# Two DMAs at the seam between attention and the za product: the last attention store on SyncE's queue, and the first gate loads ahead of two bulk loads

## The chip, the cores and the metric

The kernel runs on one core of a Trainium2 chip. The core has TensorE (PE, matrix products), VectorE (DVE, elementwise work), ScalarE (ACT, activations and copies), GpSimd (POOL) and SyncE (SP), each with its own in-order stream of instructions, and 16 DMA engines that all of them feed. DMAs are issued here by SyncE and by POOL, for the most part. The metric is the time of one execution on the device, in microseconds (us), as the median of several runs.

## The reference, cut to what matters

One layer of a hybrid encoder, 1024 tokens by 1024 channels, all in float32:

```python
h = rmsnorm(x, norm_g)
q, k, v, za, u, vs, zs, gm = split(h @ w_in)
a = window_sink_attention(rope(q), rope(k), v, sinks)      # 16 heads, 2 key heads, 128-frame window
a = (a * silu(za)) @ w_att_out
s = chunked_spatial_gating(gelu(u), gelu(vs), ...)
s = (s * silu(zs)) @ w_sg_out
ga, gs = split(sigmoid(gm + b_merge))
out = rmsnorm(x + (ga * a + gs * s) @ w_o, final_g)
```

The change touches the place where the attention result `a` is handed to `a * silu(za)`.

## The kernel before, in words

**Products.** Every large product is computed with feature rows on the 128 partitions and 1024 tokens in two halves of 512. It uses Strassen's scheme on 2 by 2 blocks: seven block products for a pair of 128-row output tiles instead of eight. A value is split into a high and a low part (`wh`, `wl` for weights, `T_...h`, `T_...l` for the other operand), and each block product is 12 matmuls of 128x128 by 128x512 (`product`, L362). One call of `gemm_pair` (L371) makes one pair of output tiles: the seven products stand in the order b11, t1, t2, b21, t3, b22, t4, and behind each one a `hook()` is called, so a pair has hooks 1 to 7. Between the products ACT copies partial results out of PSUM into tiles named `x` (L380, L384, L387), DVE adds the next partial results to them (L392, L397, L401), and `split_next` splits the next weights: high part on ACT (L176), low part on DVE (L177). There are five `x` tiles in rotation, and a pair uses four.

**Stages around the change.** The products for z (the SiLU path of the gating branch), gs and ga are made first, and the attention, cut into small steps, runs from their hooks. Each of the 16 attention tiles is (g, t): half the heads g by a block of 128 tokens t. `value_stage` (L1535) ends a tile: ACT and DVE bring it into `aT` (L1559, L1560), and POOL issues its store into the DRAM scratch `at_dr` (L1562). After the last of them the memory of the attention's tiles is given back, and a new pool, `later`, is laid over it. It holds four bulk tiles `bq` of 128 x 2048 values and the gate tiles `g0`, `g1`, later also `g2`, `g3`.

Then come four pairs for za (m = 0, 2, 4, 6; two by `gemm_pair`, two by a variant that keeps partial sums in PSUM). Each of their hooks calls `part_of_s`, which does two jobs side by side:

- It makes the operand of the following product, silu(z) times the spatial gating result. `parts_of_s` (L1767) returns a schedule written out by hand: a dictionary from (m, hook) to the steps to be issued there. `load` brings a quarter of z into a bulk tile (1024 KB, `bq<-z_dr`), `load_factors` a quarter of the gating result (1024 KB, `bq<-s_dr` in the traces), `load_row` one 128-row piece of it, `silu` works on ACT (L1787), `multiply` on DVE (L1791).
- It makes the za operand. When a quarter-tile of za is complete, ACT applies SiLU (L1857). `finish_silu` (L1837) multiplies it on DVE by the matching tile of the attention result (L1744), has POOL store it to the DRAM scratch `a_dr` (L520), and asks for the next gate. A **gate** here is that tile of the attention result, read back from `at_dr` (256 KB, `g<-at_dr`) by `want_gate` (L1756) into a free gate tile. The first two are asked for by the step `first_gates` (L1803); every later one needs a gate tile that a multiply has released.

`copy_to` (L211) issues on SyncE; all loads of this stage go that way, and the instruction shown for them is L212. SyncE handles its entries in order, so a load that must wait holds up those behind it.

**What sets the order.** The program is recorded as written and then planned: for each engine a fixed order is chosen from the dependences, the order of writing and estimated durations, and semaphores are placed. `after(b, a)` (L99) adds an order by hand; the gate multiplies stand so behind the latest partial sum (`term`), and the SiLU steps behind the latest ACT copy (`pace`).

Of the kernel before, what the change touches and what calls it, by code (L numbers as in the profile page):

```python
# [52 lines left out]
def hybrid_tile(  # L53
# [16 lines left out]
    nc = tc.nc  # L70
# [12 lines left out]
    def bank(tag, dt=F32):  # L83
        return psum.tile([P, 512], dt, name=nm("ps_" + tag), tag="ps_" + tag, bufs=2)
# [14 lines left out]
    def after(second, first):  # L99

        tc.add_manual_dep(
            second.ins,
            first.ins.name,
            mybir.DependencyInfo(mybir.DependencyClass.NoSync, mybir.DependencyReason.DATA),
            reason="order",
        )
# [104 lines left out]
    def copy_to(dst, src):  # L211
        nc.sync.dma_start(dst, src)  # L212
# [39 lines left out]
    def half_of(half):  # L252
        return slice(half * HALF, (half + 1) * HALF)
# [198 lines left out]
    def of_w(i0, i1):  # L452
        return lambda dst, i, j: copy_to(dst, w[(i0, i1)[i]][:, half_of(j)])

    def of_token_w(base, m):


        def load(dst, i, j):
            first, c0 = base + 4 * ((m + i) // 4) + 2 * j, ((m + i) % 4) * P
            d = dst.rearrange("p (c k n) -> p c k n", c=2, k=2)  # L460
            for c in range(2):
                copy_to(d[:, c], w[first + c].rearrange("p (k n) -> p k n", k=2)[:, :, c0 : c0 + P])

        return load
# [8 lines left out]
    for base, step in ((W_U, 1), (W_Q, 0), (W_ZS, 1), (W_SG, 2), (W_ATT, 2)):  # L473
        if base == W_Q:
            jobs.append(pair_job(len(jobs), of_kv))
        for m in range(0, KC, 2):
            load = of_w(base + step * m, base + step * (m + 1)) if step else of_token_w(base, m)
# [44 lines left out]
    def get(src, m, half, bufs, tag="g"):  # L522
        g = mtile([P, HALF], F32, tag, bufs, pool)
        copy_to(g[:], place(src, m, half))
        return g
# [820 lines left out]
    steps = [(g, t, par) for g in range(2) for t in range(NT) for par in range(2)]  # L1346
# [61 lines left out]
    def atile(shape, dt, tag, bufs):  # L1408
        return mtile(shape, dt, tag, bufs, pool)
# [125 lines left out]
    def value_stage(g, t, par, parts):  # L1535


        if par == 0:
            keys[g, t][3] = atile([P, 4, P], F32, "aT", 2)
        _, va, vb, at = keys[g, t]  # L1540
        a, b = parts
        po = bank("o")
        vs = slice(par * HD, par * HD + P)
        first = slice(0 if t else 256, 512)
        for n in range(2):
            nc.tensor.matmul(  # L1546
                po[:, first], va[1][:, vs], a[:, n, first], start=n == 0, stop=n == 1, skip_group_check=True
            )
        for c in range(2 if t else 1):
            cs = slice(256 * c, 256 * c + 256)  # L1550
            nc.tensor.matmul(
                po[:, cs], vb[c][:, vs], b[c][:], start=t == 0, stop=True, skip_group_check=True
            )
        here, there = slice(HD * par, HD * (par + 1)), slice(HD * (1 - par), HD * (2 - par))
        out_of, dst = (
            lambda half: po[half].rearrange("p (c i q) -> p c i q", c=2, i=4),
            at[here].rearrange("p i (c q) -> p c i q", c=2),
        )
        nc.scalar.copy(dst, out_of(there))  # L1559
        nc.vector.tensor_add(dst, dst, out_of(here))  # L1560
        if par == 1:
            nc.gpsimd.dma_start(  # L1562
                at_dr[:].rearrange("(c p) t -> p c t", p=P)[:, 4 * g : 4 * g + 4, t * P : (t + 1) * P], at[:]
            )

# [2 lines left out]
    def attention():  # L1568
# [9 lines left out]
        def value(n):  # L1578
            value_stage(*steps[n], weights.pop(0))
            if n % 2 and n + 3 < len(steps):  # L1580
                value_loads(*tiles[n // 2 + 2])
# [63 lines left out]
    def bq(n=None):  # L1645
        if n is None:
            n_bq[0] += 1
        return mtile([P, 4, HALF], F32, f"bq{(n_bq[0] if n is None else n) % 4}", 1, pool)
# [92 lines left out]
    def times(v, by, minus):  # L1741
        if minus:
            return nc.vector.scalar_tensor_tensor(v, v, -1.0, by, op0=ALU.mult, op1=ALU.mult)
        return nc.vector.tensor_mul(v, v, by)  # L1744
# [11 lines left out]
    def want_gate(src, m, half):  # L1756
        tag = free_tags.pop(0)
        gates.append((tag, get(src, m, half, 1, tag)))
# [8 lines left out]
    def parts_of_s():  # L1767

        factors, of_rows = [], {}

        def rows(src, j, half):
            return src[:].rearrange("(c p) t -> p c t", p=P)[:, 4 * j : 4 * j + 4, half_of(half)]

        def load(j, half):
            s_q[j, half] = q = bq()
            copy_to(q[:], rows(z_dr, j, half))

        def load_factors(j, half):  # L1780
            factors.append(bq(0))
            copy_to(factors[-1][:], rows(s1_dr, j, half))

        def silu(j, half):
            for c in range(0, 4, 2):
                v = s_q[j, half][:, c : c + 2, :]
                after(nc.scalar.activation(v, v, AF.Silu), pace[0])  # L1787

        def multiply(j, half, c):
            v = s_q[j, half][:, c : c + 2, :]  # L1790
            after(nc.vector.tensor_mul(v, v, factors[-1][:, c : c + 2, :]), term[0])  # L1791

        def load_row(c, half):
            of_rows[c, half] = get(s1_dr, 4 + c, half, 1, f"g{2 + c % 2}")

        def multiply_row(c, half):
            v = s_q[1, half][:, c, :]
            move = times(v, of_rows[c, half][:], half == 0)
            after(move, term[0])
            if half == 0 and c > 1:  # L1800
                late_rows.append(move)

        def first_gates():  # L1803
            for _ in range(2):
                want_gate(at_dr, *of_att.pop(0))

        def more_gates():
            free_tags.extend(("g2", "g3"))
            for _ in range(2):
                want_gate(at_dr, *of_att.pop(0))  # L1810

        return {
            (0, 1): [(load, 0, 0), (load_factors, 0, 0)],
            (0, 2): [(load, 1, 1)],
            (0, 3): [(load, 0, 1), (first_gates,)],
            (0, 4): [(load_row, 0, 1), (load_row, 1, 1)],
            (0, 5): [(silu, 0, 0)],
            (0, 6): [(multiply, 0, 0, 0)],
            (0, 7): [(multiply, 0, 0, 2), (load_factors, 0, 1), (silu, 1, 1)],
            (2, 1): [(multiply_row, 0, 1), (multiply_row, 1, 1), (load_row, 2, 1), (load_row, 3, 1)],  # L1820
            (2, 3): [(silu, 0, 1)],
            (2, 6): [(multiply, 0, 1, 0), (multiply_row, 2, 1)],
            (2, 7): [(multiply, 0, 1, 2), (multiply_row, 3, 1), (load, 1, 0), (load_row, 0, 0), (load_row, 1, 0)],
            (4, 6): [(silu, 1, 0)],
            (4, 7): [(multiply_row, 0, 0), (multiply_row, 1, 0), (load_row, 2, 0), (load_row, 3, 0)],
            (6, 2): [(multiply_row, 2, 0), (multiply_row, 3, 0), (more_gates,)],
        }


    of_att = [(m + i, half) for m in range(0, KC, 2) for i, half in ORDER]  # L1830
    s_q = {}
    making_s = parts_of_s()
    of_za = [0]

# [191 lines left out]
    for p in range(4):  # L2026
        n, t, acc, x11 = N_PAIRS + p, T_ORDER[p], accs[p], firsts[p]
# [191 lines left out]
```

## Time and profile before

| | |
|---|---|
| time, median of 3 runs | 897.91 us (896.01 to 897.95) |
| span of the profiled execution | 895.1 us |
| time of the profiled execution itself | not on the page |
| PE, matmuls | 883.5 us busy (99%), 4117 matmuls |
| PE, weight loads | 730.8 us (82%) |
| DVE / ACT / POOL | 685.0 (77%) / 580.7 (65%) / 152.2 us (17%) |
| DMA | 212.40 MB, mean 237 GB/s |

The span runs from the first to the last instruction of one execution, and the time of a run is measured around it, so it is somewhat longer. A busy PE means that matmuls are under way; their ends are modelled. In the views, "a<-b" is output<-input by the names in the program, "x12" a count, and a wait is put down to whatever released it. SPq stands for SyncE's queue of DMA issues: its durations are the issue alone, not the transfer.

### The profile page before, as it was taken

Reading aid. Unit: us, or ns where it says so; the run is one execution under the profiler, and the core shown is the slowest. Engines: PE = TensorE matmul, PEld = TensorE weight load, DVE = VectorE, ACT = ScalarE, POOL = GpSimd, SP = SyncE. Lnnn points to the kernel's source line nnn. Section 1 sums busy time; section 2 is a strip of 40 time slices with the busy share of each in tenths; the row PEclk is TensorE's granted clock in tenths of the full one; section 3 lists DMA queues with packets and bytes.
Section 4 is the critical chain, followed back from the end, with each engine's and each line's share of the span. In section 5 each row is a group of like instructions: output and inputs, shape, how many; then the busy total and the mean of one; then the engine's idle time right before and its main releaser. Section 6 shows DMA issues by size and latency. Waiting matters only on the chain.

```text
span 895.1 us, 13162 instructions
## 1 busy us (share of the span) xinstructions
PE 883.5 (99%) x4117; PEld 730.8 (82%) x4117; DVE 685.0 (77%) x1362; ACT 580.7 (65%) x1189; POOL 152.2 (17%) x218
## 2 busy tenths in 40 slices
PE   9999999999999999999999999999999999999997
PEld 6888888888888888888888888887888888888886
DVE  7879966566686778888878888846796588479886
ACT  6875523334445489999989999964685375467443
POOL 3322222203030011111211011101121121110012
PEclk9999999999999999999999999999999999999999
DMA  9998888858778767887776689989899789998523
GB/s 333 216 280 207 270 202 172 172 159 266 245 247 299 205 186 188 210 196 192 179 234 216 228 225 229 243 297 336 313 286 385 284 227 255 307 294 283 189 105 131
DMA packets 130962, 212.40 MB, mean 237 GB/s; under 512 B 12778, under 2 KB 59370, under 8 KB 130892
## 3 DMA queue, kind: packets, MB, share of 16 engines
q1 hardware_dynamic: 108280, 148.36, 49.9%
q0 software_dynamic: 22464, 62.93, 31.4%
q8 instruction: 33, 0.54, 0.2%
q14 instruction: 37, 0.30, 0.1%
q10 hardware_dynamic: 148, 0.27, 0.1%
HBM read 146.37 MB, written 86.11 MB: 260 GB/s over the span
## 4 chain that ended last, share of the span: by engine, by line
PE 90%; issue 3%; ACT 3%; DMA 2%; DVE 1%; SPq 0%; POOL 0%; ACTq 0%; POOLq 0%
PE ps_mm L362 39%; PE ps_o L362 25%; PE ps_tp L362 6%; PE ps_sc L362 3%; PE ps_o L793 3%; PE ps_tp L793 2%; PE ps_mm L793 2%; PE ps_sc L1438 2%; PE ps_tp L1511 2%; PE ps_tp L1109 2%; PE ps_o L1546 2%; PE ps_sc L793 1%; DMA a_dr<-x 1%; DMA wr<-in_x_dram 1%; PE ps_sc L663 1%
## 5 line engine op out<-in xcount | busy, mean ns | idle before, releaser
L176 ACT CAST wh<-s 128x1024 fp32r<-128x1024 f32 (+1 forms) x79 | 79.4, 1007 | 75.9 <-PE ps_mm L362 27.6
L177 DVE TENSOR_TENSOR wl<-wr,wh 128x512 fp32r<-128x512 f32 (+1 forms) x77 | 72.1, 938 | 60.0 <-ACT wh L176 59.1
L177 DVE TENSOR_TENSOR wl<-s,wh 128x1024 fp32r<-128x1024 f32 (+1 forms) x79 | 92.6, 1173 | 9.7 <-ACT wh L176 9.5
L176 ACT CAST wh<-wr 128x512 fp32r<-128x512 f32 (+1 forms) x77 | 63.0, 819 | 54.6 <-PE ps_mm L362 31.6
L362 PE MATMUL ps_o<-T_t1h,wh 128*128 128x512 f32 x148 | 57.8, 391 | 0.0
L362 PE MATMUL ps_o<-T_t1h,wl 128*128 128x512 f32 x148 | 57.7, 390 | 0.0
L362 PE MATMUL ps_o<-T_t1l,wh 128*128 128x512 f32 x148 | 57.6, 389 | 0.0
L362 PE MATMUL ps_mm<-T_t3h,wh 128*128 128x512 f32 x140 | 55.0, 393 | 2.0 <-ACT x L387 2.0
L1444 ACT COPY sl<-ps_sc 128x384 f32<-128x384 f32 (+2 forms) x128 | 51.8, 456 | 7.0 <-DVE sm L1450 7.0
L1466 ACT ACTIVATE pr<-pr,sm 128x192 f32<-128x192 f32 (+2 forms) x128 | 56.2, 443 | 0.1
L1450 DVE CUSTOM_DVE_ANT_0 pr<-sl,nsink_sb 128x192 f32<-128x192 f32 (+2 forms) x128 | 48.1, 400 | 10.0 <-ACT sl L1444 8.9
L362 PE MATMUL ps_mm<-T_b11h,wh 128*128 128x512 f32 x140 | 55.0, 393 | 0.0
L362 PE MATMUL ps_mm<-T_b11l,wh 128*128 128x512 f32 x140 | 54.6, 390 | 0.0
L362 PE MATMUL ps_mm<-T_t3h,wl 128*128 128x512 f32 x140 | 54.6, 390 | 0.0
L362 PE MATMUL ps_mm<-T_b11h,wl 128*128 128x512 f32 x140 | 54.6, 390 | 0.0
L362 PE MATMUL ps_mm<-T_t2l,wh 128*128 128x512 f32 x140 | 54.6, 390 | 0.0
L362 PE MATMUL ps_mm<-T_t3l,wh 128*128 128x512 f32 x140 | 54.6, 390 | 0.0
L362 PE MATMUL ps_mm<-T_t2h,wh 128*128 128x512 f32 x140 | 54.6, 390 | 0.0
L362 PE MATMUL ps_mm<-T_t2h,wl 128*128 128x512 f32 x140 | 54.5, 389 | 0.0
L362 PE MATMUL ps_mm<-T_t4h,wh 128*128 128x512 f32 x136 | 53.4, 393 | 0.0
L362 PE MATMUL ps_mm<-T_t4h,wl 128*128 128x512 f32 x136 | 53.1, 390 | 0.0
L362 PE MATMUL ps_mm<-T_t4l,wh 128*128 128x512 f32 x136 | 53.0, 389 | 0.0
(425 smaller groups left out, 2455.0 us busy)
## 6 DMA issues: line engine op xcount, KB each, us to landing
wr<-in_w_dram SPq DMA_DIRECT2D x86, 256.0 KB
sums<-in_w_dram POOLq DMA_DIRECT2D x20, 512.0 KB, 6.7
s<-sums SPq DMA_DIRECT2D x20, 512.0 KB
q_hl<-qhl SPq DMA_DIRECT2D x16, 512.0 KB
q<-q_hl SPq DMA_DIRECT2D x64, 128.0 KB
y_dr<-x POOLq DMA_DIRECT2D x28, 256.0 KB, 6.7
g<-in_w_dram POOLq DMA_DIRECT2D x12, 512.0 KB, 6.0
wr<-in_w_dram SPq DMA_DIRECT2D x11, 512.0 KB
```

Source lines behind the costliest of these rows:

```text
L176: hi_of.append(nc.scalar.copy(hi, src))
L177: lo_of.append(nc.vector.tensor_sub(lo, src, hi.bitcast(F32)))
L362: nc.tensor.matmul(acc, lt, rt, start=fresh and k == 0 and n == 0, stop=k == 3 and n == 2, skip_group_check=True,)
L663: turns.append(nc.tensor.transpose(pt[:, i * P : (i + 1) * P], xt[:, k * P : (k + 1) * P], ident[:]))
L793: mm = nc.tensor.matmul(acc[:], lt, rt, start=fresh and k == 0 and n == 0, stop=stops and k == 3 and n == terms[-1], skip_group_check=True,)
L1109: nc.tensor.matmul(pm[:, t * P : (t + 1) * P], xh[:, half * 4 + t, g * P : (g + 1) * P], bias[-1][1][:, g % 4, :], start=True, stop=True,)
L1438: nc.tensor.matmul(sc, q_of[:, c, i * P : (i + 1) * P], kt[:, :, lo:hi], start=True, stop=True)
L1444: copies.append(nc.scalar.copy(two, sc))
L1450: nc.vector.tensor_tensor_reduce(v, two[:, 0, :], two[:, 1, :], 1.0, nsk[:, i : i + 1], op0=ALU.add, op1=ALU.min, accum_out=nmax[:, c, i : ...
L1466: e = nc.scalar.activation(v, v, AF.Exp, bias=nmax[:, c, i : i + 1], scale=-1.0, accum_out=sums[:, c, i : i + 1])
L1511: nc.tensor.transpose(dst, pr[:, i, block * P : block * P + width], ident[:])
L1546: nc.tensor.matmul(po[:, first], va[1][:, vs], a[:, n, first], start=n == 0, stop=n == 1, skip_group_check=True)
```

## The change

Two edits. The store of the last attention tile, (g, t) = (1, 7), is issued by SyncE and no longer by POOL; the other fifteen stay on POOL. And in the schedule of the first za pair the step `first_gates` moves from hook 3, behind the load of the z quarter (0, 1), to hook 2, ahead of the load of the z quarter (1, 1). On SyncE's queue the order z(0,0), factors, z(1,1), z(0,1), gate, gate becomes z(0,0), factors, gate, gate, z(1,1), z(0,1), with the store ahead of all of them. No data and no arithmetic change.

```diff
@@ value_stage
         nc.scalar.copy(dst, out_of(there))
         nc.vector.tensor_add(dst, dst, out_of(here))
         if par == 1:
-            nc.gpsimd.dma_start(
+            (nc.sync if (g, t) == steps[-1][:2] else nc.gpsimd).dma_start(
                 at_dr[:].rearrange("(c p) t -> p c t", p=P)[:, 4 * g : 4 * g + 4, t * P : (t + 1) * P], at[:]
             )
@@ parts_of_s
         return {
             (0, 1): [(load, 0, 0), (load_factors, 0, 0)],
-            (0, 2): [(load, 1, 1)],
-            (0, 3): [(load, 0, 1), (first_gates,)],
+            (0, 2): [(first_gates,), (load, 1, 1)],
+            (0, 3): [(load, 0, 1)],
             (0, 4): [(load_row, 0, 1), (load_row, 1, 1)],
             (0, 5): [(silu, 0, 0)],
```

## The prediction

> **What bounds the kernel now.** I read the page first, then the waits of TensorE (PE), then the chain of waits around the edit, then the timelines of that stretch.
>
> ```profile
> span 895.1 us, 13162 instructions
> ...
> PE 883.5 (99%) x4117; PEld 730.8 (82%) x4117; DVE 685.0 (77%) x1362; ACT 580.7 (65%) x1189; POOL 152.2 (17%) x218
> ```
>
> PE is busy for 883.5 of 895.1 us. An edit that takes no product away can win only some of the other 11.6 us. The waits of PE, longest first:
>
> ```profile
> PE ps_mm L362 <- ACT x L387: 2.0, 1, 2.0
> PE ps_sc L565 <- POOL eps_sb L115: 1.0, 1, 1.0
> ```
>
> The longest is one wait of 2.0 us, and it lies behind the edited lines. The chain of waits there:
>
> ```profile
> 583.90 0.78 POOL at_dr L1562
> ...
> 605.24 0.55 POOL a_dr L520
> ...
> 605.91 6.87 DMA a_dr<-x
> ...
> 612.88 0.59 ACT x L387
> ...
> 613.52 3.04 PE ps_mm L362 x12
> 616.56 2.72 PE ps_o L362 x12
> ```
>
> Read it backwards: PE waits for an ACT copy (L387) into an x buffer; the copy waits until the old content of that buffer, a gated za tile, has landed in a_dr; that store left POOL only at 605.9. The PE timeline prices the wait:
>
> ```profile
> 611.12 0.39 PE L362 MATMUL ps_tp<-T_b21h,wl 128*128 128x512 f32 x1
> 613.52 0.50 PE L362 MATMUL ps_mm<-T_t3h,wh 128*128 128x512 f32 x1 [2.01 <-ACT x L387]
> ...
> 616.39 0.39 PE L362 MATMUL ps_o<-T_b22h,wh 128*128 128x512 f32 x1
> ```
>
> Matmuls start every 2.72 / 12 = 0.23 us, so the one at 613.52 was due at 611.12 + 0.23 = 611.35: **2.17 us lost**. The product behind the wait took 616.39 - 613.52 = 2.87 instead of 2.72: another 0.15. Together 2.3 us are at stake.
>
> Why did the store leave so late? The timelines of VectorE (DVE) and of SyncE's queue (SPq):
>
> ```profile
> 582.20 1.40 DVE L1560 TENSOR_TENSOR aT<-aT,ps_o 64x512 f32<-64x512 f32 x2
> ...
> 597.95 0.69 DVE L401 TENSOR_TENSOR x<-x,ps_o 128x512 f32<-128x512 f32 x1 [2.04 <-PE ps_o L362]
> 598.55 1.22 DVE L1791 TENSOR_TENSOR bq<-bq,bq 128x1024 f32<-128x1024 f32 x1
> 599.69 1.22 DVE L177 TENSOR_TENSOR wl<-s,wh 128x1024 fp32r<-128x1024 f32 x1
> 600.82 1.22 DVE L1791 TENSOR_TENSOR bq<-bq,bq 128x1024 f32<-128x1024 f32 x1
> 604.24 1.37 DVE L1744 TENSOR_TENSOR x<-x,g 128x512 f32<-128x512 f32 x2 [2.20 <-DMA g<-at_dr]
> ```
>
> ```profile
> 582.31 0.55 SPq L212 DMA_DIRECT2D s<-sums  x1
> 588.89 0.37 SPq L212 DMA_DIRECT2D bq<-z_dr  x1
> 589.31 0.50 SPq L212 DMA_DIRECT2D bq<-s_dr  x1
> 589.86 1.22 SPq L212 DMA_DIRECT2D bq<-z_dr  x2
> 591.13 2.64 SPq L212 DMA_DIRECT2D g<-at_dr  x2
> ```
>
> The two gate multiplies (L1744) begin at 604.24, when the first gate lands, although DVE was free from 602.04. The gates were issued at 591.13, behind four bulk loads (the two z loads at 589.86 stand on one row) that began only at 588.89. Sizes, by the DMA issues from 575 to 640:
>
> ```profile
> bq<-z_dr SPq DMA_DIRECT2D x4, 1024.0 KB
> s<-sums SPq DMA_DIRECT2D x6, 512.0 KB
> g<-at_dr SPq DMA_DIRECT2D x12, 256.0 KB
> ```
>
> So two things made the gate late, and the change touches both.
>
> **Part 1, the last attention store, from POOL to SyncE.** What SyncE waited for before 588.89, and what its store took:
>
> ```profile
> SPq L212 <- DMA at_dr<-aT: 5.8, 1, 5.8
> ```
>
> ```profile
> DMA to landing us min/median/max: 4.8/4.8/4.8
> ```
>
> (The second row is the store issued at 583.90 alone: landed at 583.90 + 4.8 = 588.7, and the first bulk load goes 0.2 us later, since its buffer lies where aT lay.) On SyncE the store can go when L1560 ends, 582.20 + 1.40 = 583.6; SyncE's last issue ended at 582.31 + 0.55 = 582.9, so it is free. That is 0.3 us earlier. Nothing useful queues behind its new wait: the next entry is the load that waits for this landing anyway. POOL loses an entry and has nothing to do until 605.2. But the 512 KB that SyncE issued at 582.31 may still be moving; from POOL the store moved beside them, from SyncE it may have to stand behind them. No row shows this store from SyncE. All sixteen from POOL:
>
> ```profile
> DMA to landing us min/median/max: 3.6/5.0/8.1
> ```
>
> Taken as bounds: landing 583.6 + 3.6 = 587.2 (1.5 us won) to 583.6 + 8.1 = 591.7 (3.0 us lost). I take 4.8 again, the row of the same bytes beside the same traffic: **0.3 us won**, no more than the earlier issue.
>
> A sentence aside: the Trainium skill (DMA: Bandwidth & Descriptors, "Issuing engines are not separate DMA queues") says that DMAs of all issuers end on the same 16 engines and that another issuer saves only the issue itself; by it this part is worth the difference of the issues, some tenths, as by my row. The same page's "Queues, rings and completion order" has a ring consumed in order, which speaks against the move: by it the store stands behind all of those 512 KB, and the sum would go towards the losing bound.
>
> **Part 2, the gates ahead of two bulk loads.** Nothing is added; two gate loads of 256 KB pass two z loads of 1024 KB. What the DMA engines moved there:
>
> ```profile
> 588.00:592.00 4.00, 4.00 (x19) 3.33 (x18) 0.69 (x1) 1.11 (x2) 0.00 (x0) 1.00 0.44 130
> 592.00:596.00 4.00, 4.00 (x20) 3.30 (x19) 2.60 (x3) 3.02 (x4) 0.00 (x0) 1.00 1.04 397
> 596.00:600.00 4.00, 4.00 (x19) 3.31 (x18) 2.05 (x3) 3.95 (x5) 0.00 (x0) 1.00 1.05 385
> 600.00:604.00 4.00, 4.00 (x19) 3.32 (x18) 2.04 (x2) 3.52 (x5) 0.00 (x0) 1.00 1.05 385
> ```
>
> The last columns are the busy share of the DMA engines and GB/s: they are full from 592 on, and the first gate lands 2.1 us after the 4.46 MB up to and with it were moved (below), which is an order kept. Two z loads are 2.10 MB; at 390 GB/s that is 5.4 us. The first gate then lands at 604.2 - 5.4 - 0.3 = **598.5**, the second 0.26 MB / 390 = 0.7 later.
>
> The passed z loads come 0.52 MB / 390 = 1.3 us later, less 0.3. What covers this: by the sums of the rows (0.52, 2.11, 3.65, 5.19 MB at the four ends) the first of them had its 3.15 MB moved at 598.7, and now its 3.67 MB at 600.05 - 0.3 = 599.8. By the same sums the first gate's 4.46 MB were moved at 602.1, so it took 2.1 us from moved to usable, and this load is usable at 601.9. Its SiLU on ACT, and what stands behind it:
>
> ```profile
> 601.93 2.00 ACT L1787 ACTIVATE bq<-bq 128x1024 f32<-128x1024 f32 x2
> 603.82 0.57 ACT L380 COPY x<-ps_mm 128x512 f32<-128x512 f32 x1
> ```
>
> The cover is used up but holds. If it fails, the copy L380 queued behind the SiLU slides; it ends at 604.39, and the next product into its bank starts one product (2.72) after this one, at 605.9, so another 1.5 us are free before PE pays:
>
> ```profile
> 603.19 0.39 PE L362 MATMUL ps_o<-T_t1h,wh 128*128 128x512 f32 x1
> ```
>
> **From gate to PE.** Each engine runs a fixed order, planned when the kernel is built; the trace does not show where the new plan puts the gate multiplies. Two cases. (a) Order kept: they follow L1791 at 602.04 instead of 604.24, 2.2 us earlier. (b) The plan sees the gates early and puts them around L401: at 598.5 and about 599.8. The two a_dr stores follow at 603.0 and 603.7, or at 599.2 and 600.5. Their landing before:
>
> ```profile
> L520 POOL DMA_DIRECT2D a_dr<-x x2: 552/552/552, 605.2 to 605.9; - x2
> ...
> DMA to landing us min/median/max: 3.6/5.2/6.9
> ```
>
> With 6.9 the second lands at 610.6 (a) or 607.4 (b). L387 needs 0.59 + 0.05 us before PE's 611.35, so a landing by 610.7 suffices: **the stall goes in both cases**. In (b) 3.3 us are to spare, enough even for the losing bound of part 1; in (a) nothing is. What is late next? No other PE wait in the page's span is over 1.0 us, and the chain after 613.52 is PE product after PE product. From there the end moves with PE.
>
> **Sum:** -2.17 (stall) - 0.15 (slow restart) + 0 (z loads, covered) + 0 (store, only slack) = -2.3 us. The page gives the profiled execution's span, 895.1, which becomes 892.8. Its own time is not given; the median of the runs, 897.91, lies 2.8 above the span, and I keep that: **895.6 us**.
>
> **Rivals.**
>
> *Stores meet fuller queues.* The stores to a_dr now go out while the DMA share is still 1.05. The row of all sixteen:
>
> ```profile
> DMA to landing us min/median/max: 3.5/6.7/11.0
> ```
>
> At 11.0 the second lands at 611.5 in (b): 0.8 of stall stays, 896.4. In (a) it lands at 614.7 instead of 612.8, 1.9 lost: 899.8. For it: 11.0 occurs. Against: the median is 6.7, and the bulk loads end sooner, too.
>
> *Slower: the multiplies block the split.* In case (b) DVE waits for the gate ahead of L177 at 599.69, which splits the weights that PE's product at 603.2 needs. Behind the gate come L1744, L401, L1744, L1791 and L177, by their start distances 0.6 + 0.6 + 0.6 + 1.15 + 1.22 = 4.2 us. It decides from a gate later than 603.2 - 4.2 = 599.0, and costs more than the 2.3 won from 601.3. If the gate comes no sooner than before (604.2), PE loses 5.2 and wins 2.3: 897.9 + 2.9 = 900.8. For it: my 598.5 is only 0.5 ahead of that point, and the store's losing bound brings it to 601.8. Against: the queue worked its loads off at an even rate, so the 5.4 us should come.
>
> *Given back.* The stall goes, but a later gate or weight load, bound by DMA and not by PE, takes 1.5 to 2.3 us in its place: 897.2 to 897.9. For it: the DMA share is still 1.05 at the end of the rows above. Against: in PE's waits no load stands as the releaser.
>
> *The change does not act.* The plan keeps the old order on SyncE or on DVE behind something else: 897.9. Nothing in the profile speaks for it; the gates had no wait of their own at 591.13.
>
> **How the numbers follow.** Forecast (stall gone, 895.6): 0.66. Fuller queues: 0.10. Given back: 0.08. Slower by the split: 0.08. No action: 0.08. A measurement of this kernel tells some 0.3% from no change: 2.7 us, and the runs shown spread over 1.9. The forecast's 2.3 us is just inside, so of its 0.66 about half an allowance for spread goes to faster, 0.30, and 0.36 to same. With the rivals: faster 0.31, same 0.59, slower 0.10. Range: 895.6 less the spread of 1.9 gives 893.7; above, no action plus a little gives 898.4. The likeliest alone: 893.7 to 896.9.
>
> **What would show it.** Right: SyncE issues the gates directly behind the s_dr load; L1744 starts before 602.1; the first a_dr stores leave before 604; no wait of PE for L387; the products from 611 on follow at 2.72. Wrong: a wait of PE near 603 for L177's wl; an a_dr store that takes over 9 us; SyncE's first z load later than 589; a new PE wait between 613 and 670. If the gate still lands at 604, the in-order account of the queue is wrong.

## The result, and the profile after

The changed kernel takes 894.85 us, the median of 22 runs (894.09 to 896.37). The kernel before, run beside it, takes 895.96 us (22 runs, 894.68 to 899.28). The ratio is 0.9985, with a 95% interval of 0.9979 to 0.9991: **0.8 to 1.9 us faster, most likely 1.1 to 1.3**, half of the 2.3 us forecast. The ratios of this document are worked out from all runs of both kernels and are not quotients of the medians. The means differ by 896.43 - 894.94 = 1.5 us. The change is smaller than the 0.3% spread that the prediction reckoned with, but the interval lies wholly on the faster side. The profiled execution of the changed kernel took 894.85 us.

The page of the changed kernel, span and busy times:

```profile
span 893.0 us, 13163 instructions
...
PE 883.5 (99%) x4117; PEld 731.3 (82%) x4117; DVE 684.9 (77%) x1362; ACT 581.0 (65%) x1189; POOL 151.4 (17%) x217
```

The same matmuls and the same PE time, in a span that is 2.1 us shorter. What PE waited for in the changed kernel (in total, times, longest):

```profile
PE ps_sc L565 <- POOL eps_sb L115: 1.0, 1, 1.0
PE ps_o L362 <- DVE aT L1560: 0.6, 3, 0.2
PE ps_o L1546 <- DVE x L392: 0.5, 1, 0.5
PE ps_o L793 <- DVE wl L782: 0.4, 1, 0.4
```

The wait for L387, 2.0 us before and the longest, is gone, and none has come in its place. In the chain of waits of the changed kernel this stretch is PE alone, each product in 2.72 us:

```profile
603.23 2.72 PE ps_o L362 x12
605.95 2.72 PE ps_mm L362 x12
608.67 2.72 PE ps_tp L362 x12
611.39 2.72 PE ps_mm L362 x12
```

The last of these four is the product that stood at 613.52 before. Why it is on time is seen on SyncE's queue of the changed kernel:

```profile
582.19 0.55 SPq L212 DMA_DIRECT2D s<-sums  x1
583.50 0.37 SPq L1562 DMA_DIRECT2D at_dr<-aT  x1
588.68 0.37 SPq L212 DMA_DIRECT2D bq<-z_dr  x1
589.10 0.50 SPq L212 DMA_DIRECT2D bq<-s_dr  x1
589.64 1.18 SPq L212 DMA_DIRECT2D g<-at_dr  x2
590.87 0.99 SPq L212 DMA_DIRECT2D bq<-z_dr  x2
```

The attention store (L1562) goes out on SyncE, and the two gates leave directly behind the factors, 1.5 us sooner and, what counts, ahead of 2 MB. VectorE in the same stretch:

```profile
595.10 0.69 DVE L397 TENSOR_TENSOR x<-x,ps_mm 128x512 f32<-128x512 f32 x1 [0.63 <-PE ps_mm L362]
599.04 0.69 DVE L1744 TENSOR_TENSOR x<-x,g 128x512 f32<-128x512 f32 x1 [3.25 <-DMA g<-at_dr]
599.65 0.68 DVE L401 TENSOR_TENSOR x<-x,ps_o 128x512 f32<-128x512 f32 x1
600.25 0.68 DVE L1744 TENSOR_TENSOR x<-x,g 128x512 f32<-128x512 f32 x1
600.85 1.22 DVE L1791 TENSOR_TENSOR bq<-bq,bq 128x1024 f32<-128x1024 f32 x1
601.98 1.22 DVE L177 TENSOR_TENSOR wl<-s,wh 128x1024 fp32r<-128x1024 f32 x1
```

This is the prediction's case (b): the first multiply stands ahead of L401. VectorE waits 3.25 us for the gate, and all that is queued behind it waits too. The split L177 ends at 601.98 + 1.22 = 603.20; PE's product that wants it starts at 603.23 in the chain above. So the margin against the "slower" rival was nothing, in this execution. GpSimd's stores and ACT's copy follow:

```profile
600.03 0.57 POOL L520 DMA_DIRECT2D a_dr<-x  x1 [21.52 <-DVE x L1744]
601.22 0.54 POOL L520 DMA_DIRECT2D a_dr<-x  x1 [0.63 <-DVE x L1744]
```

```profile
608.48 0.62 ACT L176 CAST wh<-wr 128x512 fp32r<-128x512 f32 x1 [1.51 <-PE ps_mm L362]
609.00 0.58 ACT L387 COPY x<-ps_mm 128x512 f32<-128x512 f32 x1
```

L387 has no wait of its own any more: it runs behind another ACT operation, ends at 609.58, and PE needs it at 611.39.

So the mechanism acted as forecast, in this pair of profiles down to the 2.17 + 0.15 us. The question is why the time moved by only about half of that.

### The profile page after: what moved, and what is told of

It reads as the page before. It is cut to its first block, busy times and chain, and to the rows that moved or that the text cites. A ratio compares the mean times of both kernels' runs of the same rounds, so it can differ in the third digit from the quotient of the medians.

```text
span 893.0 us, 13163 instructions
## 1 busy us (share of the span) xinstructions
PE 883.5 (99%) x4117; PEld 731.3 (82%) x4117; DVE 684.9 (77%) x1362; ACT 581.0 (65%) x1189; POOL 151.4 (17%) x217
## 4 chain that ended last, share of the span: by engine, by line
PE 93%; ACT 3%; DVE 2%; issue 1%; DMA 1%; POOL 0%; SPq 0%; ACTq 0%
PE ps_mm L362 41%; PE ps_o L362 26%; PE ps_tp L362 7%; PE ps_sc L362 3%; PE ps_tp L793 2%; PE ps_o L793 2%; PE ps_mm L793 2%; PE ps_sc L1438 2%; PE ps_tp L1511 2%; PE ps_tp L1109 2%; PE ps_o L1546 2%; PE ps_sc L793 1%; PE ps_o L1551 1%; PE ps_sc L663 1%; ACT pr L1466 1%
## 5 line engine op out<-in xcount | busy, mean ns | idle before, releaser
L177 DVE TENSOR_TENSOR wl<-wr,wh 128x512 fp32r<-128x512 f32 (+1 forms) x77 | 72.0, 937 | 56.1 <-ACT wh L176 55.2
L177 DVE TENSOR_TENSOR wl<-s,wh 128x1024 fp32r<-128x1024 f32 (+1 forms) x79 | 92.5, 1170 | 9.6 <-ACT wh L176 9.6
L362 PE MATMUL ps_o<-T_t1h,wh 128*128 128x512 f32 x148 | 57.9, 391 | 0.0
L362 PE MATMUL ps_o<-T_t1h,wl 128*128 128x512 f32 x148 | 57.7, 390 | 0.0
L362 PE MATMUL ps_o<-T_t1l,wh 128*128 128x512 f32 x148 | 57.6, 389 | 0.0
L362 PE MATMUL ps_mm<-T_b11h,wh 128*128 128x512 f32 x140 | 55.0, 393 | 0.0
L362 PE MATMUL ps_mm<-T_t3h,wh 128*128 128x512 f32 x140 | 54.9, 392 | 0.0
L362 PE MATMUL ps_mm<-T_b11l,wh 128*128 128x512 f32 x140 | 54.6, 390 | 0.0
L362 PE MATMUL ps_mm<-T_t3h,wl 128*128 128x512 f32 x140 | 54.6, 390 | 0.0
L362 PE MATMUL ps_mm<-T_b11h,wl 128*128 128x512 f32 x140 | 54.6, 390 | 0.0
L362 PE MATMUL ps_mm<-T_t2l,wh 128*128 128x512 f32 x140 | 54.6, 390 | 0.0
L362 PE MATMUL ps_mm<-T_t2h,wh 128*128 128x512 f32 x140 | 54.6, 390 | 0.0
L362 PE MATMUL ps_mm<-T_t3l,wh 128*128 128x512 f32 x140 | 54.6, 390 | 0.0
L362 PE MATMUL ps_mm<-T_t2h,wl 128*128 128x512 f32 x140 | 54.5, 389 | 0.0
L362 PE MATMUL ps_mm<-T_t4h,wh 128*128 128x512 f32 x136 | 53.5, 393 | 0.0
L362 PE MATMUL ps_mm<-T_t4h,wl 128*128 128x512 f32 x136 | 53.1, 390 | 0.0
L362 PE MATMUL ps_mm<-T_t4l,wh 128*128 128x512 f32 x136 | 53.0, 389 | 0.0
```

Of the source, the lines that this page charges most:

```text
L177: lo_of.append(nc.vector.tensor_sub(lo, src, hi.bitcast(F32)))
L362: nc.tensor.matmul(acc, lt, rt, start=fresh and k == 0 and n == 0, stop=k == 3 and n == 2, skip_group_check=True,)
```

## The experiments

Two theories stood at the start. **A**: the wait for L387 varies from execution to execution, and 2.17 us was one execution's. **B**: it is worth 2.2 us every time, and the changed kernel spends half of the gain again, near 603, behind the multiplies that wait for the gate.

### Each part alone

```diff
@@ store alone (value_stage)
-            nc.gpsimd.dma_start(
+            (nc.sync if (g, t) == steps[-1][:2] else nc.gpsimd).dma_start(
@@ gates alone (parts_of_s)
-            (0, 2): [(load, 1, 1)],
-            (0, 3): [(load, 0, 1), (first_gates,)],
+            (0, 2): [(first_gates,), (load, 1, 1)],
+            (0, 3): [(load, 0, 1)],
```

> Part 1 alone: the last attention store on SyncE, the gates where they were; no engine but POOL and SyncE gets another order. In the profile of the changed kernel the first z load went only 0.07 us earlier against PE than before, so theory A (the wait of PE for L387 is what the change removes; it varies from execution to execution and is typically some 1.2 us, the 2.17 us was one execution's) and theory B (the wait is worth 2.2 us in every execution, and the changed kernel spends half of it again near 603, behind the gate multiplies) both expect no change: ratio 0.9995 to 1.0005, and the wait of PE for L387 still there. A rival on part 1, that the store itself wins the time: ratio 0.9985.

> Part 2 alone: the gates ahead of the two z loads, the store on POOL. Theories A and B both expect all of the change's gain, ratio 0.9985, no wait of PE for L387, gate multiplies at about 599. If part 1 matters: ratio 0.999 or above.

The store alone: 896.15 us beside 895.84 of the kernel before, ratio 0.9998 [0.9985, 1.0011]: no gain. (A loss of 0.3 us, which is met further down, would not stand out in this interval.) The wait stays; waits of PE with the store alone:

```profile
PE ps_mm L362 <- ACT x L387: 1.7, 1, 1.7
```

The gates alone: 894.54 us, ratio 0.9984 [0.9976, 0.9993], and no wait for L387. The gates are the whole gain.

### The wait taken away by other means

The second za pair uses the variant that keeps partial sums in PSUM, which leaves the L387 of that pair out. The partial sums of this pair are then other values, so its result is not the reference's; the amount of work on PE is the same.

```diff
-        if m < 4:
+        if m < 2:
             gemm_pair(hb, finish, lambda: part_of_s(m), "tp")
```

> Neither part of the change. The second za pair keeps its partial sums in PSUM, as the third and fourth do, so its copy (now L426) does not wait for a store to land in a_dr; one DVE add falls away. The gates stay late, so nothing new stands ahead of the weight split. This prices the wait of PE by itself. Theory A: 1.0 to 1.4 us, ratio 0.9985 to 0.9989, as the change. Theory B: 2.2 us, ratio 0.9975. Given back later (a wait bound by DMA): ratio near 1.0, and the span's end no earlier although the wait is gone.

Measured: 894.29 us, ratio 0.9984 [0.9973, 0.9995], the same as with the gates ahead. Removing the wait without moving a gate is worth what the change is worth. That speaks against a half given back near 603, where this kernel has the old order, but not beyond doubt: its profiled execution has a new wait later, at 665, `PE ps_mm L362 <- ACT ps_tp L418: 1.4, 1, 1.4`. That execution took 897.13 us and is the slowest of the twelve, whose median is 2.8 us lower, so what a typical one pays there is not seen.

### The gates ahead of everything

```diff
-            (0, 1): [(load, 0, 0), (load_factors, 0, 0)],
-            (0, 2): [(first_gates,), (load, 1, 1)],
+            (0, 1): [(first_gates,), (load, 0, 0), (load_factors, 0, 0)],
+            (0, 2): [(load, 1, 1)],
```

> The change, with the two gates ahead of the first z load and the factors too. The gates then land some 5 us sooner (about 594), before the multiply has its turn at 595.8, so DVE does not wait for a gate and the split L177 ends at about 600.9 again, 2.3 us ahead of PE's need. Theory A: 0.2 us better than the change at most, ratio 0.9982 to 0.9986. Theory B: the 1.1 us spent near 603 come back, ratio 0.9973.

Measured: 895.08 us, ratio 0.9991 [0.9981, 1.0001]. No wait for L387, no new wait over 1.0 us. Another 2 MB of head start brings nothing, as it must if the copy already has time to spare. The estimate misses theory A's 0.9982 to 0.9986 by a little, though its interval takes them in; theory B's 0.9973 lies outside.

### The kernel before, three more profiles

No edit.

> The kernel before, unchanged, profiled once more: how long does TensorE wait for L387 (2.17 us in the profile before)? Theory A (the wait varies from execution to execution, typically some 1.2 us): a wait that lies somewhere from 0.5 to 2.2 us and differs from its two sisters by more than 0.3 us. Theory B (2.2 us in every execution): 2.0 to 2.3 us here and in both sisters.

> Second of three profiles of the kernel before. Theory A: a wait for L387 of 0.5 to 2.2 us, not the same as in the first. Theory B: 2.0 to 2.3 us.

> Third of three profiles of the kernel before. Theory A: mean of the three waits for L387 near 1.2 us. Theory B: mean 2.0 to 2.3 us.

The matmul behind the wait, in the PE timelines of the three, in order (their executions took 894.63, 897.59 and 895.14 us):

```profile
611.16 0.50 PE L362 MATMUL ps_mm<-T_t3h,wh 128*128 128x512 f32 x1 [0.67 <-ACT x L387]
```

```profile
612.63 0.65 PE L362 MATMUL ps_mm<-T_t3h,wh 128*128 128x512 f32 x1 [1.97 <-ACT x L387]
613.08 0.63 PE L362 MATMUL ps_mm<-T_t3l,wh 128*128 128x512 f32 x1
613.50 0.63 PE L362 MATMUL ps_mm<-T_t3h,wl 128*128 128x512 f32 x1
...
616.38 0.39 PE L362 MATMUL ps_mm<-T_t3h,wh 128*128 128x512 f32 x1
```

```profile
611.76 0.50 PE L362 MATMUL ps_mm<-T_t3h,wh 128*128 128x512 f32 x1 [0.93 <-ACT x L387]
```

With the first profile's 2.01 the same wait of the same program was 2.01, 0.67, 1.97 and 0.93 us. Theory A holds: mean 1.4, and the wait that the prediction worked from was the longest of the four. Most of the difference lies in the landing of the second a_dr store, 6.9, 5.9, 7.1 and 6.3 us behind its issue in the four.

The second one shows something that neither theory had. Behind its wait the matmuls start every 0.43 us and not every 0.23, until 616.4. The windows of that execution, from 608 on (PE, PEld, DVE, ACT, POOL busy, then the granted clock, the DMA share and GB/s):

```profile
608.00:612.00 4.00, 2.65 (x12) 1.88 (x10) 1.98 (x3) 0.90 (x3) 1.08 (x2) 1.00 0.88 219
612.00:616.00 4.00, 3.37 (x8) 2.67 (x9) 0.56 (x1) 3.94 (x5) 0.00 (x0) 0.60 1.04 405
616.00:620.00 4.00, 4.00 (x18) 3.27 (x17) 1.96 (x3) 0.82 (x2) 0.54 (x1) 0.97 0.98 372
```

The granted clock falls to 0.60 in the four microseconds behind the wait. The product took 4.60 us in place of the 3.02 to 3.04 that it took behind the other waits: another 1.6 us. Spans agree: from the matmul behind the wait to the end it is 892.8 - 611.16 = 281.6 in the first, 893.4 - 611.76 = 281.6 in the third, 895.1 - 613.52 = 281.6 in the profile before, and 895.8 - 612.63 = 283.2 here.

So one execution of the kernel before loses its wait, 0.3 us around it (3.03 - 2.72; the prediction has the same 0.3 as 0.15 of slow restart and as 2.17 lost where the wait is 2.01), and now and then 1.6 us of clock. Over the four profiles that is (2.01 + 0.67 + 1.97 + 0.93) / 4 + 0.3 + 1.6 / 4 = **2.1 us in the mean, and 1.75 in the median** without the clock. Four are too few to fix it better, and one fall of the clock in four is probably too many: the mean granted clock of the second execution is 0.996 and that of the other three 0.998 to 0.999, and of the 71 runs of the kernel before that stand beside the experiments, five show 0.996 and six 0.997. With 5 to 11 falls in 71 the clock costs 0.1 to 0.25 us in the mean, and the whole 1.8 to 1.95 us, as an estimate.

### A late gate with the multiplies ahead

The transfers of the kernel before, but VectorE's order is nearly that of the changed kernel: the first gate multiply ahead of L401, the second ahead of the split L177. (L1791, which in the changed kernel stands between the second multiply and the split, came out behind the split.) This builds the "slower" rival, at a somewhat lower price.

```diff
-        after(times(q[:], next_gate()[:], m >= KC // 2 and half == 0), term[0])
+        by_gate = times(q[:], next_gate()[:], m >= KC // 2 and half == 0)
+        after(by_gate, term[0])
+        by_gates.append(by_gate)
...
+        if of_za[0] == 6:
+            after(term[0], by_gates[0])
+            after(lo_of[-1], by_gates[1])
```

> The transfers of the kernel before (first gate landing near 604.2 us), but VectorE has the two first gate multiplies (L1744) ahead of the drain L401 and the weight split L177 of the first half's end, as the changed kernel has them. If the prediction's slower rival is right about the mechanism, L177 now ends 3.1 us behind the gate at 604.2 (in the changed kernel it ended 603.20 with the gate at 599.04 and 0.6 of that was not waiting), near 607.9 us, and TensorE, whose product wants that weight at 603.1, waits 4 to 5 us there, while its wait for L387 at 613 is gone: net 2.5 to 4 us slower than before, ratio 1.003 to 1.0045. If VectorE's order is harmless (L177 is made before the product needs it, or the wait is given back), ratio 0.998 to 1.001 and no wait of TensorE over 1 us between 600 and 610.

Measured: 897.97 us beside 896.09, ratio 1.0014 [1.0005, 1.0024]: slower than the kernel before. VectorE, and the chain from there:

```profile
604.01 0.69 DVE L1744 TENSOR_TENSOR x<-x,g 128x512 f32<-128x512 f32 x1 [7.87 <-DMA g<-s_dr]
604.62 0.68 DVE L401 TENSOR_TENSOR x<-x,ps_o 128x512 f32<-128x512 f32 x1
605.22 0.69 DVE L1744 TENSOR_TENSOR x<-x,g 128x512 f32<-128x512 f32 x1
605.82 1.22 DVE L177 TENSOR_TENSOR wl<-s,wh 128x1024 fp32r<-128x1024 f32 x1
```

```profile
605.90 1.14 DVE wl L177
607.05 0.04 issue
607.09 4.14 PE ps_o L362 x10
611.23 2.74 PE ps_mm L362 x12
```

The rival's mechanism is real: VectorE stands idle for 7.87 us, the split ends at 607.04, and PE waits for it. The wait is 1.9 us and not the 4 to 5 expected, for two reasons: the split does not stand behind L1791 and ends at 607.04 in place of 607.9, and PE makes seven matmuls first (7 x 0.23 = 1.6 us), two of its product that do not need the split and five of a later one. Ten matmuls behind the wait take 4.14 us in place of 2.27. Of these 1.9 us some 0.3 are the restart seen above and 1.6 the clock (granted 0.63 from 608 to 612). The expected ratio of 1.003 or more was missed for the first two reasons.

### The gates later still

```diff
-            (0, 3): [(load, 0, 1), (first_gates,)],
-            (0, 4): [(load_row, 0, 1), (load_row, 1, 1)],
+            (0, 3): [(load, 0, 1)],
+            (0, 4): [(load_row, 0, 1), (load_row, 1, 1), (first_gates,)],
```

> The kernel before with its first two gate loads put one step later still, behind the two row loads of s (512 KB more), so that the gate lands near 605.5 us in place of 604.2, with VectorE's gate multiplies, the store of a_dr and L387 behind it. If the gate's landing sets the store and the store sets L387, TensorE's wait for L387, 0.7 to 2.0 us in four profiles of the kernel before, becomes 2 to 3.3 us: 1.3 us more. If on top of that a gap of about 2 us or more halves TensorE's granted clock for some 3.6 us (it did behind a gap of 1.97 us in the second profile of the kernel before, granted clock 0.60 from 612 to 616, and behind 1.93 us in the kernel with the late gate ahead, but not behind 1.98 us in the first profile of the kernel before), another 1.6 to 1.9 us, and the clock falls in every execution: 2.5 to 3.5 us slower than the kernel before, ratio 1.0028 to 1.004. Without the clock: 1.3 us slower, ratio 1.001 to 1.002. If the gate's landing isn't what sets the wait: ratio 0.999 to 1.001 and a wait as before.

Measured: 898.01 us beside 895.64, ratio 1.0017 [1.0003, 1.0031]. The multiplies, the wait and the windows of its profile:

```profile
605.33 1.37 DVE L1744 TENSOR_TENSOR x<-x,g 128x512 f32<-128x512 f32 x2 [0.56 <-DMA g<-at_dr]
```

```profile
PE ps_mm L362 <- ACT x L387: 2.8, 1, 2.8
```

```profile
612.00:616.00 4.00, 1.95 (x5) 1.56 (x6) 0.45 (x1) 2.58 (x4) 0.09 (x1) 0.72 0.95 282
616.00:620.00 4.00, 4.00 (x17) 3.21 (x16) 2.51 (x3) 2.00 (x3) 0.00 (x0) 0.85 1.03 404
```

The wait is 0.8 us longer than the longest seen before. The sum fits: counted from SyncE's last store ahead of the stage (`ga_dr<-x`, 581.30 here and 581.55 in the first profile), the multiplies start 1.3 us later, and the second a_dr store lands 6.32 us behind its issue in place of 6.87. The chain from the gate to L387 is so shown from both sides. The clock fell in this execution too, but the ratio lies where only the wait counts. Of the ten runs, five have a mean granted clock of 0.996 or 0.997 and took 897.8 to 899.5 us, the other five 0.998 or 0.999 and 894.4 to 898.2. So the clock does not seem to fall every time.

### The changed kernel again, and with the split ahead of the multiplies

Two more profiles of the changed kernel, and a variant in which the split L177 goes ahead of both gate multiplies:

```diff
+        if of_za[0] == 6:
+            for by_gate in by_gates:
+                after(by_gate, lo_of[-1])
```

> The changed kernel profiled again. Theory A (the wait for L387 is what varied, the changed kernel has no such wait in any execution): no wait of TensorE over 1.1 us in the whole span, none for L387, for the weight split L177 or for a gate between 600 and 616 over 0.3 us, and the time from the start of the first za product to the last TensorE instruction 304.6 to 305.0 us, as in its first profile (304.69). Theory B (it spends part of the gain again near 603 in some executions): a wait of 0.5 us or more for L177 near 603.

> Second of two further profiles of the changed kernel. Theory A: no wait for L387 or L177 over 0.3 us, za stage 304.6 to 305.0 us. Theory B: at least one of the two shows 0.5 us or more at L177.

> The changed kernel with VectorE's first two gate multiplies (L1744) ordered behind the weight split L177 that TensorE needs at 603.2, so that this split, which ended 603.20 in the changed kernel, ends near 600.9. Theory A (the split is in time in the changed kernel, no loss there): the time of the changed kernel, ratio to the kernel before 0.998 to 0.999. Theory B (part of the gain is lost in some executions by this split): better than the changed kernel, ratio 0.9970 to 0.9978.

Neither profile has a wait for L387 or L177. VectorE's first multiply in the two:

```profile
597.71 0.69 DVE L1744 TENSOR_TENSOR x<-x,g 128x512 f32<-128x512 f32 x1 [1.27 <-DMA g<-at_dr]
```

```profile
597.35 0.69 DVE L1744 TENSOR_TENSOR x<-x,g 128x512 f32<-128x512 f32 x1 [1.42 <-DMA g<-at_dr]
```

The gate comes sooner than in the first profile, and the split ends at 602.04 and 602.13, 1.8 and 1.2 us before PE's product starts at 603.88 and 603.36. The variant, whose split ends 2.4 us before PE's product (599.69 + 1.22 = 600.91, against 603.35), took 894.13 us, ratio 0.9986 [0.9975, 0.9997]: no better than the changed kernel. Theory B expected 0.9970 to 0.9978, which only the edge of this interval touches.

A count from ahead of the change decides between the theories. SyncE's last store before this stage (of the ga product, issued for L520) is untouched by the change. In the profile before and in the first one of the changed kernel it is:

```profile
581.55 0.32 SPq L520 DMA_DIRECT2D ga_dr<-x  x1
```

```profile
581.43 0.32 SPq L520 DMA_DIRECT2D ga_dr<-x  x1
```

From this store to the start of VectorE's last instruction (L2065, shown below) the changed kernel takes 306.69, 306.68 and 306.69 us in its three profiles, and 306.70 with the split first: making the split sooner gains nothing. The kernel before takes 309.02, 307.66, 310.55 and 307.93 us, that is 2.3, 1.0, 3.9 and 1.2 us more, its four waits with what follows them. So theory B falls. The store itself goes out at 580.5 to 582.1 us in the fourteen profiles; that spread lies ahead of the change. No variant here beats the changed kernel by more than the intervals.

## Point by point

**What bounds the kernel: right.** PE's 883.5 us stayed, and the one wait that was worth taking is the one that went.

**The stall: right mechanism, wrong size.** This is the step that failed: "2.17 us lost" was read from one execution and set against a median of others. The wait of the kernel before is 0.67 to 2.01 us, and the profiled execution was at its top. The "another 0.15" held wherever the clock stayed up: 2.87, 2.86 and 2.87 us for that product. By the waits above the change takes away some 1.7 us in a typical execution.

**The store: slack, as taken, but the 0.3 us was not won, and a small cost was missed.** On SyncE the store leaves 0.27 us sooner (2.08 us behind the `ga_dr` store, against 2.35). Counted from there, the first load behind it goes after 7.0 us in the mean of the six profiles with the store on SyncE (6.8 to 7.25), and after 7.1 in the eight with it on POOL (6.6 to 7.4): no difference. From the store's issue to that load pass 4.9 us in the mean from SyncE and 4.7 from POOL. In the Trainium skill (DMA: Bandwidth & Descriptors, "Queues, rings and completion order") rings are consumed in order, and by that rule the store would have stood behind the 512 KB of 582.2; the traces show 0.2 us of it in the mean, less than their spread, and agree with "Issuing engines are not separate DMA queues" of the same page, that no more than the issue is saved.

What was missed lies at the end of the kernel. VectorE's last instruction (L2065, in the chains) in the kernel before, with the gates alone, with the store alone, and in the changed kernel, whose spans are 895.1, 893.2, 895.2 and 893.0 us:

```profile
890.57 0.75 DVE bq L2065
```

```profile
888.64 0.75 DVE bq L2065
```

```profile
890.29 0.75 DVE bq L2065
```

```profile
888.12 0.75 DVE bq L2065
```

That is 895.1 - 890.57 = 4.5 and 893.2 - 888.64 = 4.6 us with the store on POOL, and 895.2 - 890.29 = 4.9 and 893.0 - 888.12 = 4.9 us with it on SyncE. In all fourteen profiles it is 4.5 to 4.6 without the moved store (eight) and 4.8 to 4.9 with it (six). **The moved store costs 0.3 us at the very end.** It lies in SyncE's closing wait for the output stores, in the kernel before and in the changed one:

```profile
SPq L2215 <- DMA out_dram<-bq: 2.0, 1, 2.0
```

```profile
SPq L2215 <- DMA out_dram<-g: 2.3, 1, 2.3
```

All eight profiles with the store on POOL have the first form and 2.0 us, all six with it on SyncE the second and 2.3 us. (The line is L2221 where the kernel is six lines longer.) Why SyncE then ends on another store was not tried.

**The gates: right.** Predicted 598.5; the first multiply started at 599.04, 597.71 and 597.35 in three profiles, against 602.86 to 604.24 in the four profiles before. That fits loads worked off in the order of issue, as assumed. Case (b) came true, and L387 was free well before PE wanted it.

**The z loads: covered, as taken.** No wait of PE for L380 or a SiLU appears.

**The sum.** 1.75 us (median of the waits with what is around them) - 0.3 us (end) = 1.4 us. Counted from the `ga_dr` store it is 1.8 - 0.3 = 1.5 as the median of the four. In the mean it is 1.8 to 1.95, less 0.3, so 1.5 to 1.65 us, and the means of the 22 runs differ by 1.5. The measured interval is 0.8 to 1.9 us. The forecast's 2.3 lies outside it, these lie inside.

**The time.** 895.6 was forecast and 894.85 came, in the range, with some luck, since two errors of opposite sign met. The forecast was 0.75 too high although the gain was overestimated, since its base was too high by more: the 2.8 us from span to time was a guess across two executions. Where both are known they lie 1.8 us apart (894.85 and 893.0; 894.63 and 892.8; 897.59 and 895.8). The profiled execution of before so took about 896.9, and the median of three that was shown, 897.91, lies 2 us above the median of 22.

**The rivals.** *Slower by the split*: its point of decision, a gate at 599.0, was met within 0.04 us in the first profile with no loss, and with a late gate it does cost more than it saves. Its price of 900.8 was too high as far as was tried: the kernel that builds it, without L1791 in the way, is 0.5 to 2.2 us slower than before, not 2.9, since other matmuls fill part of the gap and the wait won is smaller. *Stores meet fuller queues*: in the first profile both a_dr stores land 6.3 us behind their issue, where the two took 3.6 and 6.9 before, so the first met fuller queues and it cost nothing. *Given back* (where 895.6 + 1.5 is 897.1 and not 897.2), *does not act*: no row shows them.

## What to carry to other kernels

A wait in a profile is one draw: before a wait of one or two microseconds is priced, profile the same kernel three or four times, and take the median of the wait, not the one that was seen. A transfer moved ahead in a queue also moves its consumer in the plan of another engine, so ask what is queued behind that consumer and by when it is needed; nearly the same order of VectorE was harmless with the gate at 599 and cost PE 1.9 us and, in the profile, its clock with the gate at 604. Compare executions from an event just ahead of the change and not from the start of the span, which lay up to 1.6 us off here. Set span to span and time to time, and never one execution's span to other executions' median.

## What the runs showed of the hardware

**A wait of 2 us can halve TensorE's clock.** Behind gaps of 1.97 us (kernel before, second of the three profiles), 1.93 us (late gate ahead) and 2.8 us (gates later) matmuls started every 0.43 us for some 2.5 to 3.5 us, and each cost 1.4 to 1.6 us more. Behind gaps of 2.01 us (first profile of before), 1.7 us (store alone), 1.4 us (the wait taken away), 0.93 and 0.67 us they did not. So near 2 us it went either way. The Trainium skill (TensorE: Matmul & The Clock Gate, "What's actually happening") has the clock fall after an idle window of about 3.4 us, in windows that run freely of the kernel, and return after as long a busy one. The rate and the length of the slow stretch agree with these rows; that a gap must be 3.4 us long does not, since 1.93 us sufficed.

**The end of this kernel goes with the queue that an early store used.** The 0.3 us above belong to a store issued 300 us before the end: SyncE's closing wait is 2.3 us for one output store where SyncE issued that early store, and 2.0 us for another where POOL did. The cause is open.
